# Rotary angles of the first layer: a transfer of their own, VectorE in place of GpSimd, and six matrix products on ones at the start

## The chip, the core and the metric

The kernel runs on one core of a Trainium2 chip. The metric is the device time of one execution in microseconds (us), the median of several runs. The engines are named as the profile names them: PE is TensorE's matmul, PEld its weight load, DVE is VectorE, ACT is ScalarE, POOL is GpSimd, SP is SyncE; a q behind a name is that engine's sequencer, which issues DMAs.

## The reference, cut to what matters

Four residual layers run over 256 positions of width 1024. A layer is a token mixer (layers 0 and 3: dilated attention in three head groups; layer 1: short convolution; layer 2: Conformer convolution) and a gated convolutional feed-forward block, each between RMS norms. The change touches only what feeds the rotary embedding of the attention layers:

```python
inv_freq = ROPE_THETA ** (-jnp.arange(0, ROT_DIM, 2, dtype=jnp.float32) / ROT_DIM)   # 8 frequencies
ang = positions.astype(jnp.float32)[..., None] * inv_freq                            # (256, 8)
cos, sin = jnp.cos(ang)[:, :, None, :], jnp.sin(ang)[:, :, None, :]
q = rope_partial(qkv[:, :, 0], cos, sin)
k = rope_partial(qkv[:, :, 1], cos, sin)
```

The angles reach 255 radians, so the kernel brings them into the range from -pi to pi before it takes sines.

## The kernel before

Activations stand transposed: 128 channels in partitions, 256 positions in the free dimension, eight such blocks (k = 0 to 7) for the width of 1024. Every fp32 product with a weight is made of three single-pass products (`mm3`, lines 280 to 282; in `value`, lines 894 to 896): high part of the weight with high and low part of the activation, low part of the weight with the high part.

**Weights** come as one stream (`Stream`): blocks `raw` of 1 MB, in three buffers, loaded by SP in the order of use (`load`; the first block in two halves). A block holds two pieces of 128x1024. ACT copies a piece to its high part `whi` (`first`, line 192), DVE subtracts to get the low part `wlo` (`second`, line 198). `st.copy()` and `st.diff()` place one such step each in the program; `take` hands the next piece to PE. A raw buffer is loaded anew when DVE has taken both of its pieces.

**Order.** All work is under a manual schedule: every engine runs its instructions in the order in which the code below issues them, and waits where an input is missing. A DMA also signals on one of eight counters, which the transfers share in turn: before SP issues a transfer, it waits until the earlier transfer on the same counter has landed. The order listings call the counters DMAHW0 to DMAHW7.

**The start** (lines 1112 to 1127): ACT's queue issues the first norm gains `par` and the positions `pi`; SP's queue issues the input `h`, the first weight blocks, the constants `cst` (identity, a block of 1/1024 named `ones`, and the 8 frequencies `freq` in the last columns), two more weight blocks, the masks `msk` and the other parameters.

**Layer 0, first steps.** `attention` (line 810) calls `rotary()`, then `boundary`, then `sines()`.

- `rotary` (line 1053) sets two tables to 1 and 0 on POOL and then does the angles, all on POOL: positions to fp32 (line 1068), times the frequencies (two instructions at line 1066), then three range steps (for e in 20, 10, 0) of eleven instructions each, 128x16 elements, each one dependent on the one ahead of it, and a clamp.
- `boundary` (line 356; here with `mg` None) makes high and low parts of the gained input: `hi` on ACT (line 291), `lo` on DVE (line 288). Between and behind them it places copies and diffs of the first weight pieces, and the squares for the norm (ACT, line 379). In the end DVE sums the squares (line 285, three sums of 128x512) and forms `acc` (line 288).
- `sines` (line 1089): two small DVE instructions (lines 288 and 1091), eight ACT sines (line 1095), a table load (line 1098).
- PE does four `column`s of 24 products (q and k of two head groups), then `value` (line 882): 24 products for the first 128 positions, and then the hook `before`: `rstd_of([acc])` (two products at line 306, whose result gives the norm factor by way of DVE and ACT), `turned` (four transposes of the tables at line 1104, copied to `ctab` and `stab` by ACT), and after it the 24 products for the other 128 positions, and the next column.

In each layer the feed-forward block then runs on PE as one long row of products (22 x 2 columns of 24, 14 slabs of 24, 8 tails of 24: 1,584 products).

## Time and profile before

| What | us |
|---|---|
| median of 3 runs | 1566.38 |
| the three runs | 1560.3, 1566.38, 1568.5 |
| the profiled execution, its own time | 1566.16 |
| its span (first to last instruction) | 1564.3 |
| around the span (1566.16 - 1564.3) | 1.86 |
| PE busy | 1538.2 (98%) |
| DVE busy | 1243.2 (79%) |
| ACT busy | 925.8 (59%) |
| POOL busy | 17.9 (1%) |

PE is busy for nearly the whole span, so a saving counts where PE stands still or runs slowly. Start times in the rows are us from the span's start. Matmuls are pipelined: how fast PE goes is read from the distance between their starts, not from how long each one lasts. `PEclk` is the granted share of TensorE's full clock, and has a value only where the trace holds a record of it.

### The profile page before, as it was taken

The numbers are of one execution on the slowest core, as the hardware profiler recorded it, in microseconds if no ns is written. First come the engines' busy times: TensorE is split into PE (matmuls) and PEld (weight loads), VectorE is DVE, ScalarE is ACT, GpSimd is POOL, SyncE is SP. The second block draws the span as 40 slices with busy tenths as digits, with TensorE's granted clock in tenths as the row PEclk, the third lists the DMA queues.
The fourth block names the chain that finished last, engine by engine and source line by source line (L and its number), as shares of the span: only waits on it lengthen the run. The fifth ranks groups of instructions, "written<-read, shape, count | busy, mean of one in ns | idle before, by whom it ended". The sixth has DMA issues, their size and how long they took to land.

```text
span 1564.3 us, 31521 instructions
## 1 busy us (share of the span) xinstructions
PE 1538.2 (98%) x13194; PEld 1501.4 (96%) x13194; DVE 1243.2 (79%) x2177; ACT 925.8 (59%) x1623; POOL 17.9 (1%) x51
## 2 busy tenths in 40 slices
PE   6999999999999999999999999999999999999998
PEld 6999999999999999999999999999999999999997
DVE  4997877698886779888699588896888778588783
ACT  6564645575574566656576666566546446565562
POOL 4000000000000000000000000000000000000000
PEclk9999999999999999999999999999999999999999
DMA  5663433266552644655333136553544334245540
GB/s 218 216 213 139 162 141 130 81 218 223 195 202 103 219 162 167 238 197 201 115 135 108 55 135 244 191 186 135 216 162 164 133 136 163 107 156 222 190 162 28
DMA packets 36718, 256.94 MB, mean 164 GB/s; under 512 B 4320, under 2 KB 4448, under 8 KB 5984
## 3 DMA queue, kind: packets, MB, share of 16 engines
q1 hardware_dynamic: 36288, 254.93, 45.2%
q8 instruction: 103, 1.69, 0.4%
q14 instruction: 39, 0.32, 0.1%
q10 hardware_dynamic: 288, 0.01, 0.0%
HBM read 253.87 MB, written 1.05 MB: 163 GB/s over the span
## 4 chain that ended last, share of the span: by engine, by line
PE 93%; DVE 3%; ACT 1%; POOL 1%; issue 1%; DMA 1%; DVEq 0%; ACTq 0%; POOLq 0%
PE psA L537 17%; PE psB L280 10%; PE psB L282 10%; PE psB L281 10%; PE psA L280 7%; PE psA L281 7%; PE psA L282 7%; PE psA L894 3%; PE psA L895 3%; PE psA L896 3%; PE psB L731 2%; PE psB L942 2%; PE psB L913 2%; PE psA L453 2%; PE psB L931 2%; PE psA L448 2%
## 5 line engine op out<-in xcount | busy, mean ns | idle before, releaser
L198 DVE TENSOR_TENSOR wlo<-raw,whi 128x1024 fp32r<-128x1024 f32 x480 | 580.2, 1220 | 34.6 <-ACT whi L192 33.9
L192 ACT CAST whi<-raw 128x1024 fp32r<-128x1024 f32 x480 | 491.1, 1049 | 22.8 <-DMA raw<-in_w_dram 17.2
L282 PE MATMUL psB<-act,wlo 128*128 128x256 f32 x1392 | 385.6, 277 | 0.0
L280 PE MATMUL psB<-act,whi 128*128 128x256 f32 x1392 | 385.6, 277 | 0.0
L281 PE MATMUL psB<-act,whi 128*128 128x256 f32 x1392 | 385.6, 277 | 0.0
L280 PE MATMUL psA<-act,whi 128*128 128x256 f32 x1040 | 298.6, 287 | 8.0 <-ACT whi L192 7.1
L282 PE MATMUL psA<-act,wlo 128*128 128x256 f32 x1040 | 290.0, 279 | 0.5 <-DVE wlo L198 0.5
L281 PE MATMUL psA<-act,whi 128*128 128x256 f32 x1040 | 290.1, 279 | 0.2
L537 PE MATMUL psA<-act,whi 128*128 128x256 f32 x1536 | 265.1, 277 | 0.0
L282 PEld LDWEIGHTS psB<-act,wlo 128*128 128x128 f32 x1392 | 262.5, 189 | 0.0
L281 PEld LDWEIGHTS psB<-act,whi 128*128 128x128 f32 x1392 | 261.3, 188 | 0.0
L280 PEld LDWEIGHTS psB<-act,whi 128*128 128x128 f32 x1392 | 261.3, 188 | 0.0
L537 PEld LDWEIGHTS psA<-act,whi 128*128 128x128 f32 x1536 | 231.7, 188 | 0.0
L537 PE MATMUL psA<-act,wlo 128*128 128x256 f32 x768 | 212.9, 277 | 0.0
L280 PEld LDWEIGHTS psA<-act,whi 128*128 128x128 f32 x1040 | 197.0, 189 | 13.6 <-ACT whi L192 7.1
L282 PEld LDWEIGHTS psA<-act,wlo 128*128 128x128 f32 x1040 | 196.9, 189 | 0.8 <-DVE wlo L198 0.8
L281 PEld LDWEIGHTS psA<-act,whi 128*128 128x128 f32 x1040 | 196.9, 189 | 0.6 <-DVE act L285 0.5
L291 ACT ACTIVATE tmp<-act,par 128x256 f32<-128x256 f32 x176 | 80.2, 503 | 161.7 <-DVE act L285 161.7
L288 DVE SCALAR_TENSOR_TENSOR tmp<-act,par,tmp 128x255 f32<-128x255 f32 (+1 forms) x352 | 146.6, 479 | 19.7 <-ACT tmp L291 19.7
L537 PEld LDWEIGHTS psA<-act,wlo 128*128 128x128 f32 x768 | 144.9, 189 | 0.0
L285 DVE TENSOR_TENSOR act<-psB,act 128x512 f32<-128x512 f32 (+2 forms) x94 | 58.5, 625 | 82.2 <-PE psB L282 45.3
L922 ACT ACTIVATE act<-act,tiny 128x512 f32<-128x512 f32 x64 | 46.4, 725 | 110.3 <-DVE tiny L920 110.3
(126 smaller groups left out, 2189.1 us busy)
## 6 DMA issues: line engine op xcount, KB each, us to landing
raw<-in_w_dram SPq DMA_DIRECT2D x239, 1024.0 KB, 4.8
h<-in_xT_dram SPq DMA_DIRECT2D x4, 256.0 KB, 5.0
raw<-in_w_dram SPq DMA_DIRECT2D x2, 512.0 KB, 5.5
out_dram<-h SPq DMA_DIRECT2D x4, 256.0 KB, 2.0
msk<-in_masks_dram SPq DMA_DIRECT2D x1, 512.0 KB, 9.4
par<-in_params_dram SPq DMA_DIRECT2D x1, 484.0 KB, 10.1
cst<-in_consts_dram SPq DMA_DIRECT2D x1, 132.0 KB, 5.9
par<-in_params_dram ACTq DMA_DIRECT2D x1, 4.0 KB, 2.9
```

Source lines behind the costliest of these rows:

```text
L192: self.nc.scalar.copy(out=hi, in_=raw)
L198: self.nc.vector.tensor_tensor(out=lo, in0=raw, in1=hi.bitcast(F32), op=ALU.subtract)
L280: nc.tensor.matmul(o, lhsT=whi, rhs=x[0], start=first, stop=False)
L281: nc.tensor.matmul(o, lhsT=whi, rhs=x[1], start=False, stop=False)
L282: nc.tensor.matmul(o, lhsT=wlo, rhs=x[0], start=False, stop=last)
L285: nc.vector.tensor_tensor(out=out, in0=a, in1=b, op=op)
L288: nc.vector.scalar_tensor_tensor(out=out, in0=a, scalar=s, in1=b, op0=op0, op1=op1)
L291: nc.scalar.activation(out=out, in_=a, func=AF.Identity, scale=s, bias=b)
L537: nc.tensor.matmul(o, lhsT=a, rhs=b, start=first and i == 0, stop=last and i == 2, skip_group_check=True)
L894: nc.tensor.matmul(oc, lhsT=xh, rhs=whi[:, k % 4, :], start=k == 0, stop=False)
L895: nc.tensor.matmul(oc, lhsT=xh, rhs=wlo[:, k % 4, :], start=False, stop=False)
L896: nc.tensor.matmul(oc, lhsT=xl, rhs=whi[:, k % 4, :], start=False, stop=k == KD - 1)
```

## The change

The frequencies get a third small transfer on ACT's queue; the transfer of `cst` on SP's queue leaves them out. The small tiles of the angles no longer come from the pool `tmp` but from a new tile `rot`. POOL still does the conversion and the two products with the frequencies. The three range steps and the clamp go to DVE. A product and a sum that were two POOL instructions are one on DVE (`STT`), so that a range step has seven instructions. The two small DVE instructions of `sines` go with the clamp. The whole is now a generator of four portions of 7, 7, 7 and 3 instructions; `boundary` calls it four times, each time behind one `st.diff()`. At the very beginning DVE sets a new tile `idle` to one, and PE does six fp32 products of 128x256 on it, whose result nobody reads.

```diff
--- before.py
+++ after.py
@@ -38,6 +38,7 @@
 FIRST = 10
 EVERY = 3
 LAG = 8
+HEAD = 6
 NCST = 2 * P + ROT // 2
 
 PCOLS = {}
@@ -245,6 +246,7 @@
     ident = cst[:, 0:P]
     ones = cst[:, P:2 * P]
     freq = cst[:, 2 * P:NCST]
+    rot = cp.tile([P, 8 * (ROT // 2)], F32, name="rot")
     msk = cp.tile([P, 2, 512], F32, name="msk")
     h2 = [cp.tile([P, 2, T], F32, name=f"h{k}") for k in range(KD // 2)]
     h = [h2[k // 2][:, k % 2, :] for k in range(KD)]
@@ -353,7 +355,7 @@
     def bc2(a):
         return a.rearrange("p (s t) -> p s t", s=1).to_broadcast([P, 2, T])
 
-    def boundary(mg, rb, gain, permuted=False):
+    def boundary(mg, rb, gain, permuted=False, beside=None):
 
 
         xs = [None] * KD
@@ -397,6 +399,7 @@
                 st.copy()
                 square(q)
                 st.diff()
+                next(beside)
             st.copy()
             st.diff()
         elif not gain:
@@ -808,8 +811,8 @@
     SWAP = [(i + 8) % 16 if i < 16 else i for i in range(32)]
 
     def attention(l, mg, rb):
-        sines, turned = rotary() if l == 0 else (None, None)
-        xs, acc = boundary(mg, rb, f"mpre{l}", True)
+        angles, sines, turned = rotary() if l == 0 else (None, None, None)
+        xs, acc = boundary(mg, rb, f"mpre{l}", True, angles)
         if l == 0:
             sines()
         ct, sn = act(), act()
@@ -1054,7 +1057,8 @@
 
 
         nf = ROT // 2
-        pf, ang, kf, a2 = tmp()[:, :2], tmp()[:, :2 * nf], tmp()[:, :2 * nf], tmp()[:, :2 * nf]
+        pf, ang, kf, a2 = (rot[:, i * 2 * nf:(i + 1) * 2 * nf] for i in range(4))
+        pf = pf[:, :2]
         tabs = [act()[:, :, :P] for _ in range(2)]
         for t, v in zip(tabs, (1.0, 0.0)):
             nc.gpsimd.memset(t, v)
@@ -1063,32 +1067,36 @@
 
         def TS(out, a, s1, op0, s2=None, op1=None):
             more = {} if op1 is None else {"op1": op1}
-            nc.gpsimd.tensor_scalar(out=out, in0=a, scalar1=s1, scalar2=s2, op0=op0, **more)
+            nc.vector.tensor_scalar(out=out, in0=a, scalar1=s1, scalar2=s2, op0=op0, **more)
 
         nc.gpsimd.tensor_copy(out=pf, in_=pi_)
         for c in range(2):
-            TS(ang[:, c * nf:(c + 1) * nf], freq, pf[:, c:c + 1], ALU.mult)
-        for e in (20, 10, 0):
-            period = two_pi * 2.0 ** e
-            parts, rest = [], period
-            for _ in range(3):
-                q = 2.0 ** (math.floor(math.log2(abs(rest))) - 12)
-                c = round(rest / q) * q
-                parts.append(c)
-                rest -= c
-            parts.append(float(np.float32(rest)))
-            TS(kf, ang, float(np.float32(1.0 / period)), ALU.mult)
-            TS(kf, kf, magic, ALU.add)
-            TS(kf, kf, -magic, ALU.add)
-            for c in parts:
-                TS(a2, kf, -c, ALU.mult)
-                nc.gpsimd.tensor_tensor(out=ang, in0=ang, in1=a2, op=ALU.add)
-        lim = float(np.nextafter(np.float32(math.pi), np.float32(0)))
-        TS(ang, ang, lim, ALU.min, -lim, ALU.max)
+            nc.gpsimd.tensor_scalar(out=ang[:, c * nf:(c + 1) * nf], in0=freq, scalar1=pf[:, c:c + 1], scalar2=None,
+                                    op0=ALU.mult)
+
+        def angles():
+            for e in (20, 10, 0):
+                period = two_pi * 2.0 ** e
+                parts, rest = [], period
+                for _ in range(3):
+                    q = 2.0 ** (math.floor(math.log2(abs(rest))) - 12)
+                    c = round(rest / q) * q
+                    parts.append(c)
+                    rest -= c
+                parts.append(float(np.float32(rest)))
+                TS(kf, ang, float(np.float32(1.0 / period)), ALU.mult)
+                TS(kf, kf, magic, ALU.add)
+                TS(kf, kf, -magic, ALU.add)
+                for c in parts:
+                    STT(ang, kf, -c, ang, ALU.mult, ALU.add)
+                yield
+            lim = float(np.nextafter(np.float32(math.pi), np.float32(0)))
+            TS(ang, ang, lim, ALU.min, -lim, ALU.max)
+            STT(a2, ang, -1.0, ang, ALU.mult, ALU.max)
+            TS(a2, a2, -1.0, ALU.mult, math.pi / 2, ALU.add)
+            yield
 
         def sines():
-            STT(a2, ang, -1.0, ang, ALU.mult, ALU.max)
-            nc.vector.tensor_scalar(out=a2, in0=a2, scalar1=-1.0, scalar2=math.pi / 2, op0=ALU.mult, op1=ALU.add)
             for t, a, sign in zip(tabs, (a2, ang), (1.0, -1.0)):
                 for half in range(2):
                     for r in range(2):
@@ -1107,13 +1115,19 @@
                 nc.scalar.copy(out=tab[:, 1, :], in_=oi)
                 scaled(tab[:, 0, :], oi, -1.0 / math.sqrt(DH))
 
-        return sines, turned
+        return angles(), sines, turned
 
     with tc.manual_schedule():
         pi_ = cp.tile([P, 2], I32, name="pi")
         nc.scalar.dma_start(out=par[:, 0:KD], in_=params[:, 0:KD])
         nc.scalar.dma_start(out=pi_, in_=pos)
+        nc.scalar.dma_start(out=freq, in_=consts[:, 2 * P:NCST])
         nc.scalar.preload_act_table(AF.Sin)
+        idle = act()
+        nc.vector.memset(idle, 1.0)
+        o = psum("B")[:, :T]
+        for _ in range(HEAD):
+            nc.tensor.matmul(o, lhsT=idle[:, 0, :P], rhs=idle[:, 1, :], start=True, stop=True)
         nc.sync.dma_start(out=h2[0], in_=xT[0])
 
         def rest():
@@ -1121,7 +1135,7 @@
                 nc.sync.dma_start(out=h2[q], in_=xT[q])
 
         st.load(1, rest)
-        nc.sync.dma_start(out=cst, in_=consts)
+        nc.sync.dma_start(out=cst[:, :2 * P], in_=consts[:, :2 * P])
         st.load(3)
         nc.sync.dma_start(out=msk, in_=masks)
         nc.sync.dma_start(out=par[:, KD:], in_=params[:, KD:])
```

What stands in a row on DVE before, from the last low part of the input on: five diffs of weight pieces, the sums of the squares, and then the two instructions of `sines` (tmp_102 is the angle tile) and the first one of the norm factor.

```order
L288 SCALAR_TENSOR_TENSOR act_170<-h_77,par,act_170 128x256
L198 TENSOR_TENSOR wlo<-raw,whi 128x1024 x5
L285 TENSOR_TENSOR act_177<-act_177,act_186 128x512
L285 TENSOR_TENSOR act_177<-act_177,act_193 128x512
L285 TENSOR_TENSOR act_177<-act_177,act_202 128x512
L288 SCALAR_TENSOR_TENSOR tmp_213<-act_177 128x256
L288 SCALAR_TENSOR_TENSOR tmp_104<-tmp_102 128x16
L1091 TENSOR_SCALAR tmp_104<-tmp_104 128x16
L309 RECIPROCAL tiny_359<-psS_356 128x2
```

The same place now, from the third portion on (rot holds the angles; lines 1070 and 290 are the helpers TS and STT; the two portions ahead of it read like the third):

```order
L199 TENSOR_TENSOR wlo<-raw,whi 128x1024
L1070 TENSOR_SCALAR rot<-rot 128x16 x3
L290 SCALAR_TENSOR_TENSOR rot<-rot 128x16 x4
L199 TENSOR_TENSOR wlo<-raw,whi 128x1024
L1070 TENSOR_SCALAR rot<-rot 128x16
L290 SCALAR_TENSOR_TENSOR rot<-rot 128x16
L1070 TENSOR_SCALAR rot<-rot 128x16
L199 TENSOR_TENSOR wlo<-raw,whi 128x1024
L287 TENSOR_TENSOR act_150<-act_150,act_166 128x512
L287 TENSOR_TENSOR act_150<-act_150,act_180 128x512
L287 TENSOR_TENSOR act_150<-act_150,act_196 128x512
L290 SCALAR_TENSOR_TENSOR tmp_210<-act_150 128x256
```

A portion now stands between one diff and the next, four times, ahead of the sums; the two instructions behind the sums are gone.

What stands on SP's queue at the start, before, from the second half of the first weight block on:

```order
L180 DMA raw<-in_w_dram 128x1024
L1124 DMA cst<-in_consts_dram 128x264 [waits DMAHW0_49]
L182 DMA raw<-in_w_dram 128x2048 [waits DMAHW1_49]
L182 DMA raw<-in_w_dram 128x2048 [waits DMAHW2_49]
L1126 DMA msk<-in_masks_dram 128x1024 [waits DMAHW3_49]
L1127 DMA par<-in_params_dram 128x968 [waits DMAHW4_49]
```

And now:

```order
L181 DMA raw<-in_w_dram 128x1024 [waits DMAHW0_49]
L1138 DMA cst<-in_consts_dram 128x256 [waits DMAHW1_49]
L183 DMA raw<-in_w_dram 128x2048 [waits DMAHW2_49]
L183 DMA raw<-in_w_dram 128x2048 [waits DMAHW3_49]
L1140 DMA msk<-in_masks_dram 128x1024 [waits DMAHW4_49]
L1141 DMA par<-in_params_dram 128x968 [waits DMAHW5_49]
```

The transfers stand in the same order, but one more transfer ahead of them has moved each by one counter. The first of these, which waited for nothing, now waits on a counter used by one of the first two transfers (`par` or the first `h`). Counter 2 belongs to `pi`: the transfer behind `cst` now waits for it, where before it was the one after. Counter 4, on which `msk` now waits, belongs to the frequencies.

## Rows read from the trace of the kernel before

**Rows 1.** Waits, first 50 us: engine line, releaser: us in all, times, longest.

```profile
PE psA L280 <- ACT whi L192: 7.1, 1, 7.1
...
PE psB L1104 <- ACT act L1095: 5.1, 1, 5.1
...
DVE tmp L288 <- POOL tmp L1066: 4.7, 1, 4.7
```

**Rows 2.** Windows: stretch and length, busy us of PE, PEld, DVE, ACT, POOL, PEclk, DMA.

```profile
25.00:30.00 5.00, 0.12 (x1) 0.15 (x2) 0.42 (x3) 0.80 (x8) 2.75 (x12) 0.74 0.13 52
30.00:35.00 5.00, 5.00 (x27) 4.87 (x28) 1.65 (x5) 4.94 (x10) 0.00 (x0) 0.58 0.00 0
```

**Rows 3.** Timeline, PE: start, us, engine, line, operation, tiles, count, idle before.

```profile
13.78 0.28 PE L280 MATMUL psA<-act,whi 128*128 128x256 f32 x1
...
21.60 0.28 PE L894 MATMUL psA<-whi,act 128*128 128x256 f32 x1
...
24.33 0.50 PE L306 MATMUL psS<-cst,tmp 128*128 128x1 f32 x4
29.88 1.09 PE L1104 MATMUL psB<-cst,act 128*128 128x128 f32 x4 [5.05 <-ACT act L1095]
30.62 0.56 PE L894 MATMUL psA<-whi,act 128*128 128x256 f32 x1
...
35.13 0.29 PE L280 MATMUL psA<-act,whi 128*128 128x256 f32 x1
```

**Rows 4.** Timeline, POOL, start of the kernel.

```profile
9.75 1.57 POOL L1066 TENSOR_SCALAR tmp<-cst,tmp 128x8 f32<-128x8 f32 x2 [3.38 <-DMA cst<-in_consts_dram]
...
28.49 0.20 POOL L1066 TENSOR_SCALAR tmp<-tmp 128x16 f32<-128x16 f32 x1
```

**Rows 5.** Timeline, ACT, 19 to 36 us.

```profile
19.22 1.05 ACT L192 CAST whi<-raw 128x1024 fp32r<-128x1024 f32 x1
29.20 0.96 ACT L1095 ACTIVATE act<-tmp 128x16 f32<-128x16 f32 x8 [8.93 <-DVE tiny L309]
...
33.69 1.28 ACT L869 ACT_TABLE_LOAD   x1
35.33 0.84 ACT L291 ACTIVATE act<-psA,tiny 128x256 f32<-128x256 f32 x2 [0.36 <-PE psA L896]
```

**Rows 6.** Timeline, DVE, 11 to 30 us.

```profile
11.95 1.23 DVE L198 TENSOR_TENSOR wlo<-raw,whi 128x1024 fp32r<-128x1024 f32 x1
14.05 1.22 DVE L198 TENSOR_TENSOR wlo<-raw,whi 128x1024 fp32r<-128x1024 f32 x1 [0.88 <-ACT whi L192]
...
21.45 2.16 DVE L285 TENSOR_TENSOR act<-act,act 128x512 f32<-128x512 f32 x3
23.64 0.43 DVE L288 SCALAR_TENSOR_TENSOR tmp<-act 128x256 f32<-128x256 f32 x1
28.72 0.18 DVE L288 SCALAR_TENSOR_TENSOR tmp<-tmp 128x16 f32<-128x16 f32 x1 [4.65 <-POOL tmp L1066]
28.93 0.17 DVE L1091 TENSOR_SCALAR tmp<-tmp 128x16 f32<-128x16 f32 x1
29.02 0.16 DVE L309 RECIPROCAL tiny<-psS 128x2 f32<-128x2 f32 x1
```

**Rows 7.** Timeline, PE, fp32 products of 128x256 (two records each).

```profile
295.36 1.89 PE L331 MATMUL psB<-cst 128*128 128x256 f32 x8
```

**Rows 8.** DMA issues, first 30 us: operation, count, KB each, median us to landing.

```profile
raw<-in_w_dram SPq DMA_DIRECT2D x5, 1024.0 KB, 6.3
...
pi<-in_pos_dram ACTq DMA_DIRECT2D x1, 1.0 KB, 5.0
```

**Rows 9.** Windows, a short idle of PE in layer 3.

```profile
1094.00:1098.00 4.00, 3.10 (x27) 2.90 (x25) 2.51 (x9) 1.84 (x4) 0.00 (x0) 1.00 0.00 0
```

**Rows 10.** Windows, PE in the feed-forward blocks of layers 0 and 3.

```profile
320.00:440.00 120.00, 120.00 (x1061) 120.00 (x1061) 105.28 (x169) 74.86 (x117) 0.00 (x0) 1.00 0.60 212
...
1400.00:1520.00 120.00, 120.00 (x1021) 120.00 (x1020) 101.16 (x164) 72.18 (x113) 0.00 (x0) 1.00 0.56 202
```

## The prediction, made before the changed kernel was run

> **What bounds the kernel now.** PE is busy for 98% of the span, so I first looked for the places where it is not. The waits of the first 50 us [rows 1] show two: PE's first product starts at 7.1 us, held by ACT's copy of the first weight piece, and later PE stands still for 5.1 us before the transposes of the rotary tables. Who is late there is read backwards through the rows. The transposes wait for ACT's eight sines (29.20 us), these for two DVE instructions (28.72 and 28.93), and these for POOL, whose clamp ends at 28.69 [rows 3 to 6]. DVE had nothing to do for 4.7 us before that. POOL started on the angles at 9.75, when the frequencies had landed, and took until then: 36 instructions in a chain, 34 of them on 128x16 elements from 11.4 on, 0.51 us each on average [rows 4].
>
> The idle costs more than its 5 us. Its window, 25 to 30 us, has a granted clock of 0.74, the next one 0.58 [rows 2]: in it TensorE falls from its upper level (2.4 GHz) to the lower (1.2 GHz). So the four transposes take 0.74 us from first start to the next product (29.88 to 30.62), and the 24 products behind them 4.51 us (30.62 to 35.13). The 24 products of the same kind ahead of the hook, at the full clock, took 2.73 us (21.60 to 24.33) [rows 3]. The start of the kernel looks alike: the trace has no clock record there, but from 13.78 on 93 products take 10.55 us until 24.33, 0.113 us each [rows 3], and before that they stand about twice as far apart.
>
> **The angle steps on DVE: what they cost.** The change takes 33 of the POOL instructions away and puts 22 in their place on DVE, together with the two that were there already: portions of 7, 7, 7 and 3. Each instruction depends on the one ahead. The nearest row is the pair in `sines`, of the same form and size: starts 28.72 and 28.93, so 0.21 us per dependent step; an independent one follows 0.09 us later [rows 6]. A portion of seven is 6 x 0.21 + 0.09 = 1.35 us, the last one 2 x 0.21 + 0.09 = 0.51 us.
>
> They stand between the diffs of weight pieces, where DVE waits for ACT: the first of four such waits is 0.88 us [rows 6], the others are 0.84 to 0.87. With the 0.08 us by which instructions overlap (the sums start at 21.45, the diff ahead of them ends at 21.53), there is room for 0.95 us. Three portions are too long by 0.40 us each, the fourth gives 0.40 back: the sums are late by 0.80 us. `acc` was ready at 23.64 + 0.43 = 24.07 and is now ready at 24.87. Its reader on PE, at line 306, came at 24.33 without waiting [rows 3, 6]. Now it comes at about 24.93, after a short wait of PE.
>
> Queued behind the portions on DVE are the diffs of the next pieces. PE takes them later than they are ready in each case: with PE at 0.113 us per product from 13.2 us on, the four diffs behind a portion end some 0.1 to 0.4 us before the product that reads them. That is thin, but any loss here comes out of the same wait for `acc`, not on top of it.
>
> Below this there is the case that the portions hide wholly: `acc` at 24.07, 0.8 us better. Above it stands POOL's own price, 0.51 us per instruction: portions of 3.57 and 1.53 us, `acc` later by 3 x 2.62 + 0.61 = 8.5 us. I take 0.21, since its row is the same operation on the same engine.
>
> The Trainium skill (VectorE: DVE Perf Modes, section "The DRAIN you can't avoid") says that the next VectorE instruction does not start until the pipe of the one ahead is empty, and that leaving out the wait between two gains nothing. The rows speak against that here: the independent one at 29.02 starts while the one ahead still runs until 29.10 [rows 6]. By the page every step would cost 0.21 us, the sum four times 0.12 us more, and the gain below would be 6.1 instead of 6.6 us.
>
> **What goes away.** The sines no longer wait for POOL. The fourth portion ends near 21.2 us; ACT finishes its copy at 19.22 + 1.05 = 20.27, so the sines (0.96 us) run from about 21.3 to 22.2, and the transposes are no longer held by them [rows 5]. PE's next sequence is the two products at line 306 from 24.93 (0.50 us), the transposes, and 24 products. PE's idle is now about 1 us at most. A window in layer 3 with 0.9 us of idle in 4 us still has the clock at 1.00 [rows 9], so I take the full clock: transposes 0.37, half of 0.74; products 2.73. The next column starts at 24.93 + 0.50 + 0.37 + 2.73 = 28.53, where it was 35.13: **6.6 us earlier**. If the clock fell all the same, 0.37 + 1.78 = 2.15 us of this would be lost.
>
> What is late next: ACT's copies of the tables and its table load (1.28 us, 33.69 to 34.97) come ahead of the scaling of `value`, which waited 0.36 us for PE [rows 5]. In the new order ACT copies at 22.2 + 1.28 to 24.5, takes the table copies behind the transposes at about 25.9, and ends the load near 28.4, when PE ends the products. It is a tie, worth 0.3 us at most. Behind it the order on every engine is what it was, with the same distances, and the saving stays until the end: nothing in the stream runs by an outside time, and the blocks needed next are issued before.
>
> **The transfers.** The frequencies land by a small transfer; the nearest row is `pi`, 1 KB, 5.0 us [rows 8]. Issued at about 1.6 us they land at 6.6, at 10 even if they queue twice as long. POOL's two products (1.57 us) [rows 4] are done before 11.6; DVE asks at 13.1. On SP's queue everything is moved by one counter: the second half of block 0 waits until about 3.6 us (landing of a first transfer), the second block until `pi` lands, near 6.1. Weight blocks took 6.3 us from issue to landing there [rows 8], so it lands by 12.4; ACT copies it at 13.0, ahead of the diff at 14.05 [rows 6]. `msk` and the parameters behind it wait for the frequencies, and nobody needs them before some tens of us. Cost nothing; if the second block were late by 1 us, `acc` would be late by as much.
>
> **The six products.** Eight records of such products, four of them, take 1.89 us [rows 7]; six are 12 records, 2.8 us, or 5.7 at half the clock. Behind a fill of DVE (0.72 us, the price of one 128x512 sum [rows 6]) they are over before 7.1, under PE's wait for the first copy. They let the first column run at the full clock, but its second piece is ready only at 11.95 + 1.23 = 13.18 [rows 6], so PE gains at most 0.5 us by 24.33, and `acc` is later than that. With the angle steps in, they are worth nothing, between 0 and 0.1 us.
>
> **Sum.** 1564.3 - 6.6 = 1557.7 for the span; with the 1.86 us around it **1559.6 us**, against 1566.16 for the profiled execution, which lies 0.2 us under the median.
>
> **The rivals.** *Another pace of PE in the feed-forward blocks.* In layer 0 a stretch of 120 us holds 1,061 products, in layer 3 only 1,021, both with PE without a gap and the clock at 1.00 [rows 10]: 113.1 and 117.5 ns. Layers 1 and 2 go as layer 0. Nothing in the code differs, so a stretch seems to keep the pace at which it begins. Over 1,584 products that is 7.0 us per layer, about the distance of the lowest run (1560.3) from the others. The change shifts every beginning. If layer 3 goes at the quick pace, the time is 1559.6 - 7.0 = 1552.6. If one more block goes at the slow one, it is 1566.6, no change. If two or more more go slow, it is 1573.6 and above: **slower than before**, from the second block on, and past 0.5% with little more.
>
> *DVE as slow as POOL.* At 0.51 us per step `acc` comes at 32.6, 7.7 us later than forecast, and after such an idle the clock is down, 2.15 us: 1569.4, slower. From about 0.40 us per step on the change loses. The row of 0.21 speaks against it.
>
> *The clock falls in the short wait.* 1559.6 + 2.15 = 1561.8; the window of layer 3 speaks against it.
>
> **How the numbers follow.** 0.5% of 1566 is 7.8 us, about what a measurement of this kernel can tell from no change. Chances: forecast, 1559.6 with bounds of 1558.5 and 1561: 0.47. Quick pace in layer 3: 0.22. One more slow block: 0.13. Clock falls: 0.10. Two or more slow blocks: 0.05. DVE like POOL: 0.03. Faster by over 0.5% are the quick pace and the part of the forecast with its best bound and a median that falls well, 0.12: 0.34 in all. Slower by over 0.5% is 0.04, most of the slow blocks. The rest, 0.62, is within. The range goes from 1553 (half of the quick pace left out) to 1566.5 (slow blocks left out).
>
> **What would show it.** In the profile of the changed kernel: on DVE, portions of about 1.35 us between diffs and the sums' end near 24.9; on ACT, sines near 21.3; on PE, line 306 near 24.9 with an idle of about 1 us before it, transposes right behind, the next column at 28.5, no clock below 1.00 between 14 and 40 us; 12 records of idle products over before 7.1. Wrong it is if a dependent DVE step takes much more than 0.21 us, if PE's idle at `acc` costs the clock, or if the feed-forward blocks change their pace: then the start shows the 6.6 us and the end does not.

## The result, and the profile after

| | before | after |
|---|---|---|
| runs beside each other, us | 1560.3, 1566.38, 1567.33, 1568.5 | 1550.05, 1551.44, 1551.7, 1552.87 |
| median, us | 1566.86 | 1551.57 |
| profiled execution, us | 1566.16 | 1551.44 |
| span of the profiled execution, us | 1564.3 | 1549.7 |

The ratio is 0.9922, 95% interval 0.9894 to 0.9949: the changed kernel is faster by 0.8%, more than the 0.5% that a measurement of this kernel can tell from no change (the two medians alone give 0.9902). The time lies 8.0 us under the forecast and 1.4 us under the range's low end. It lies 1.0 us under the time that the rival of the quick pace gave (1552.6).

The runs of before lie in two groups, one near 1560 us (the lower) and one near 1567.5 us (the upper), and this ratio compares a mixture of them with one group. The experiments below add 75 runs of before in four series, and the groups return in each.

**The start.** Rows of PE in the kernel after (columns as in [rows 3]):

```profile
1.45 5.49 PE L1130 MATMUL psB<-act 128*128 128x256 f32 x12 [1.45 <-DVE act L1127]
7.00 0.58 PE L282 MATMUL psA<-act,whi 128*128 128x256 f32 x1
...
24.65 0.61 PE L308 MATMUL psS<-cst,tmp 128*128 128x1 f32 x4 [0.63 <-DVE tmp L290]
25.12 0.64 PE L1112 MATMUL psB<-cst,act 128*128 128x128 f32 x4
25.51 0.36 PE L897 MATMUL psA<-whi,act 128*128 128x256 f32 x1
...
28.42 0.28 PE L282 MATMUL psA<-act,whi 128*128 128x256 f32 x1
```

The idle of 5.05 us in [rows 3] is gone; 0.63 us is left, and it stands before the products that read `acc` (line 308 now), as foretold. The transposes follow at once. The column behind `value` starts at 28.42 us where it was 35.13: 6.71 us earlier.

DVE in the kernel after (columns as in [rows 6]): a portion stands between two diffs (line 199).

```profile
11.80 1.23 DVE L199 TENSOR_TENSOR wlo<-raw,whi 128x1024 fp32r<-128x1024 f32 x1
12.94 0.58 DVE L1070 TENSOR_SCALAR rot<-rot 128x16 f32<-128x16 f32 x3
13.56 0.80 DVE L290 SCALAR_TENSOR_TENSOR rot<-rot 128x16 f32<-128x16 f32 x4
14.28 1.22 DVE L199 TENSOR_TENSOR wlo<-raw,whi 128x1024 fp32r<-128x1024 f32 x1
...
20.37 0.17 DVE L1070 TENSOR_SCALAR rot<-rot 128x16 f32<-128x16 f32 x1
20.57 0.17 DVE L290 SCALAR_TENSOR_TENSOR rot<-rot 128x16 f32<-128x16 f32 x1
20.78 0.17 DVE L1070 TENSOR_SCALAR rot<-rot 128x16 f32<-128x16 f32 x1
20.86 1.22 DVE L199 TENSOR_TENSOR wlo<-raw,whi 128x1024 fp32r<-128x1024 f32 x1
22.00 2.14 DVE L287 TENSOR_TENSOR act<-act,act 128x512 f32<-128x512 f32 x3
24.17 0.43 DVE L290 SCALAR_TENSOR_TENSOR tmp<-act 128x256 f32<-128x256 f32 x1
```

Seven steps take 1.34 us from their first start to the next diff (12.94 to 14.28). Dependent steps start 0.20 to 0.21 us apart (20.37, 20.57, 20.78), and the independent diff 0.08 us behind the last of them, while that one still runs. The Trainium skill (VectorE: DVE Perf Modes, section "The DRAIN you can't avoid") says that the next instruction does not start until the pipe is empty, and in the same paragraph that one that is not held starts earlier. The trace agrees with the second, with the 0.08 us of the diff; the prediction told only the first.

Two windows of the kernel after, one at the start and one in the last feed-forward block (columns as in [rows 2] and [rows 10]):

```profile
25.00:30.00 5.00, 5.00 (x45) 5.00 (x45) 1.82 (x6) 4.05 (x9) 0.00 (x0) 1.00 0.24 98
30.00:35.00 5.00, 5.00 (x45) 5.00 (x45) 4.58 (x5) 4.18 (x5) 0.00 (x0) 1.00 0.45 151
1400.00:1520.00 120.00, 120.00 (x1061) 120.00 (x1061) 102.90 (x166) 74.13 (x115) 0.00 (x0) 1.00 0.53 188
```

The granted clock stays at 1.00, the upper level, where [rows 2] have 0.74 and 0.58. The last window answers to the second of [rows 10]: 1,061 products in 120 us where there were 1,021. Layer 3's feed-forward block now goes at the quick pace (0.113 us per product, where the slow one is 0.118).

**Where the 14.6 us of span come from.** The same ACT instruction in both kernels, at the entry of the last feed-forward block and near its end (start, us, engine, line, operation, tiles). Kernel before:

```profile
1363.82 0.91 ACT L291 ACTIVATE act<-h,par 128x256 fp32r<-128x256 f32 x2 [2.57 <-DVE h L285]
...
1544.91 0.47 ACT L291 ACTIVATE act<-psA,par 128x256 f32<-128x256 f32 x1
```

Kernel after:

```profile
1356.52 0.91 ACT L293 ACTIVATE act<-h,par 128x256 fp32r<-128x256 f32 x2 [2.57 <-DVE h L287]
...
1530.98 0.47 ACT L293 ACTIVATE act<-psA,par 128x256 f32<-128x256 f32 x1
```

At the entry the kernel after is 7.30 us ahead, near the end 13.93. So 6.6 us were won in this block alone, where the change has no instruction. Of the 7.3 us ahead of it, 6.7 are there at 28 us. Another part, some 0.8 us by PE's starts (6.51 us ahead at 850.96, 7.28 at 862.60), is won at the end of the Conformer mixer of layer 2: there a window of before, and then the matching one of after (columns as in [rows 2]), read

```profile
866.00:871.00 5.00, 5.00 (x22) 4.31 (x22) 2.46 (x9) 3.22 (x6) 0.00 (x0) 0.66 0.01 3
```

```profile
859.00:864.00 5.00, 4.72 (x31) 4.04 (x31) 2.46 (x9) 3.51 (x7) 0.00 (x0) 1.00 0.00 0
```

The granted clock was 0.66 there before and is 1.00 after. This part need not belong to the change: e8 below, in which only the last block differs from before, has 1.00 there too, and between before and its second trace (e5) the entry of the last block moves by 2.0 us (1363.82 and 1365.80) although the column behind `value` starts at 35.13 and 35.09.

Three questions stay: which part of the change makes the 6.7 us, whether the other two are needed, and why the last block went quick.

### The profile page after: what moved, and what is told of

Read it like the earlier page. It is cut to its first block, busy times and chain, and to the rows that moved or that the text cites. A ratio compares the mean times of both kernels' runs of the same rounds, so it can differ in the third digit from the quotient of the medians.

```text
span 1549.7 us, 31536 instructions
## 1 busy us (share of the span) xinstructions
PE 1532.4 (99%) x13206; PEld 1493.1 (96%) x13206; DVE 1246.3 (80%) x2200; ACT 925.4 (60%) x1623; POOL 3.8 (0%) x17
## 4 chain that ended last, share of the span: by engine, by line
PE 94%; DVE 4%; ACT 1%; issue 1%; DMA 0%; DVEq 0%; SPq 0%; ACTq 0%
PE psA L540 17%; PE psB L284 10%; PE psB L283 10%; PE psB L282 10%; PE psA L282 7%; PE psA L283 7%; PE psA L284 7%; PE psA L897 3%; PE psA L898 3%; PE psA L899 3%; PE psB L734 2%; PE psB L945 2%; PE psB L916 2%; PE psA L456 2%; PE psB L934 2%; PE psA L451 2%
```

## The experiments

Each ratio is to runs of before in the same series, with its 95% interval, also where the edit is shown against after.

The four runs of after are quick and those of before mostly are not. Theory A at the outset: the six products take a buffer of the rotating kinds `act` and PSUM "B", so every later tile stands in another buffer, and that sets the block's pace. Theory B: the pace is set by something else, a matter of timing or chance at the block's beginning.

### e1: the products alone

Against the kernel before:

```diff
+        idle = act()
+        nc.vector.memset(idle, 1.0)
+        o = psum("B")[:, :T]
+        for _ in range(6):
+            nc.tensor.matmul(o, lhsT=idle[:, 0, :P], rhs=idle[:, 1, :], start=True, stop=True)
         nc.sync.dma_start(out=h2[0], in_=xT[0])
```

> The kernel before plus the six products on ones alone (and with them one more tile of the rotating activation tiles and one more bank B taken at the start). Start theory (what bounds is POOL's chain of angles): the columns run at the full clock, but the transposes still wait for the sines at 29.2 us, and the next column starts at 35.1 us as before; gain at the start 0. Two theories for the 7 us by which the last feed-forward block became shorter in the changed kernel (0.113 instead of 0.118 us per product): (A) the shift of the rotating tiles by one decides the pace: then this kernel has the quick pace too, 1559 to 1560 us; (B) the moment at which PE begins decides: behind 35 us this kernel runs like the one before, 1566 us.

Measured: 1559.67 us (1557.65 to 1560.74, ten runs), ratio 0.9978 [0.9958, 0.9998]. PE in e1, and its window in the last block:

```profile
23.62 0.61 PE L307 MATMUL psS<-cst,tmp 128*128 128x1 f32 x4
29.34 1.09 PE L1105 MATMUL psB<-cst,act 128*128 128x128 f32 x4 [5.12 <-ACT act L1096]
```

```profile
1400.00:1520.00 120.00, 120.00 (x1062) 120.00 (x1061) 104.11 (x170) 74.23 (x117) 0.00 (x0) 1.00 0.56 202
```

PE comes to `acc` 0.7 us earlier than in [rows 3] and then waits for the sines as before: the transposes are earlier by 0.5 us (29.34 for 29.88), the column behind by 0.2 (34.91 for 35.13). The start of before itself moves by as much (35.09 to 35.79 in e5, e8 and e11, which leave it as it was or nearly so). So the products do nothing for the start. But all ten runs lie in the lower group, and the traced one has the quick pace.

### e2: the change without the products

Against the kernel after:

```diff
-        idle = act()
-        nc.vector.memset(idle, 1.0)
-        o = psum("B")[:, :T]
-        for _ in range(HEAD):
-            nc.tensor.matmul(o, lhsT=idle[:, 0, :P], rhs=idle[:, 1, :], start=True, stop=True)
```

> The changed kernel without the six products on ones (so the rotating activation tiles and banks B stand as before; the tile for the angles and the four tmp tiles fewer stay). Start theory: the sums of squares set the end of the first stretch, not the products; the second half of the clock's ramp is hidden; line 306 still at 24.7 us, next column at 28.4 to 28.6 us, gain at the start 6.5 to 6.7 us. A rival at the start: without them the first columns run at half clock until some 13.7 us and end at 24.3, which is still ahead of the sums, so at most 0.2 us lost. Pace theory A (tiles): the last block is slow again, 1558 to 1560 us. Pace theory B (moment): it stays quick, 1551 to 1553 us.

Measured: 1553.54 us (1552.24 to 1554.29, seven runs), ratio 0.993 [0.991, 0.995]. The next column starts at 28.75, 0.33 us later than in after; the last block is quick, with 1,061 products in the window. So the products are not needed for the quick pace either. The other 1.6 us or so of the median lie between layers 1 and 3: e2's trace is 2.6 us behind after at the entry of the last block (1359.11 for 1356.52), and it has the fall of the clock at the Conformer mixer. The two traces of before differ by 2.0 us at that entry, so that these runs don't tell what the products do there.

### e3: the transfer alone

Against the kernel before:

```diff
         nc.scalar.dma_start(out=pi_, in_=pos)
+        nc.scalar.dma_start(out=freq, in_=consts[:, 2 * P:NCST])
...
-        nc.sync.dma_start(out=cst, in_=consts)
+        nc.sync.dma_start(out=cst[:, :2 * P], in_=consts[:, :2 * P])
```

> The kernel before plus the frequencies' own transfer alone; the angles stay on POOL. They land at 6.8 instead of 9.6 us, so POOL begins 2.7 us earlier and ends its clamp near 26 us; sines at 26.5, transposes near 27. If TensorE's clock still falls in the idle of some 2.4 us: next column at 32.4, gain at the start 2.7 us; if the clock holds: 30.3, gain 4.8 us. Whole time 1561 to 1563.5 us with the last feed-forward block at the slow pace, 7 us less at the quick one. Pace theory A (tiles stand as before): slow.

Measured: 1558.38 us (1557.25 to 1559.41, ten runs), ratio 0.9958 [0.994, 0.9975]. PE and one window of e3:

```profile
28.08 1.09 PE L1104 MATMUL psB<-cst,act 128*128 128x128 f32 x4 [3.50 <-ACT act L1095]
```

```profile
25.00:30.00 5.00, 1.92 (x9) 1.82 (x10) 0.42 (x3) 2.57 (x10) 1.38 (x7) 0.77 0.11 44
```

POOL starts on the angles 2.7 us earlier (7.07 for 9.75) and ends only 1.8 us earlier (26.89 for 28.69). In the stretch gained its steps stand beside a busy DVE, where single ones take longer in e9 below; that this makes the missing 0.9 us was not measured. PE still waits 3.50 us, the clock still falls, and the next column comes at 32.77, 2.36 us earlier than before. The chain on POOL is what had to go. The traced last block is quick here too, and all ten runs lie in the lower group.

### e4: the change, with the products on buffers that are there anyway

Against the kernel after:

```diff
-        idle = act()
-        nc.vector.memset(idle, 1.0)
-        o = psum("B")[:, :T]
+        nc.vector.memset(ctab, 1.0)
+        o = psum("S")[:, :T]
...
-            nc.tensor.matmul(o, lhsT=idle[:, 0, :P], rhs=idle[:, 1, :], start=True, stop=True)
+            nc.tensor.matmul(o, lhsT=ctab[:, 0, :P], rhs=ctab[:, 1, :], start=True, stop=True)
```

> The changed kernel with the six products on a tile of the tables that is free at that time and with another bank as output, so that the rotating activation tiles and the banks B stand as in the kernel before, and all times are those of the changed kernel. Start theory: next column at 28.4 us as in the changed kernel. Pace theory A (the shift by one decides): last block slow, 1558 to 1559 us. Pace theory B (the moment decides): quick, 1551 to 1552 us.

Measured: 1551.94 us (1551.11 to 1553.51, five runs), ratio 0.9922 [0.9895, 0.9949]; next column at 28.50, quick pace (1,061). `act` and "B" rotate as in before now (as in e2), and the time is that of after. Theory A falls for the changed kernel.

### e5: the kernel before once more

> The kernel before, unchanged, for a second trace and more runs on the same chip beside the others. Its 23 runs so far lie in two heaps, nine near 1559.6 us and most of the others near 1567.5 us, while each variant so far keeps to one heap. If the pace of the last feed-forward block (7 us) is what parts them, a run near 1559.6 has about 1,061 products in the 120 us from 1400 us on and one near 1567.5 has 1,021. If the heaps come from something else, a trace near 1559.6 shows 1,021 there as well.

Measured: 1559.56, 1560.03, 1560.55, 1560.6, 1561.47 and 1566.5, 1566.53, 1567.62, 1568.13, 1568.28 us; ratio 0.9999 [0.9977, 1.0021]. Five runs in each group and none in the five microseconds between them. The traced run (1568.13) has the slow pace in the last block:

```profile
1400.00:1520.00 120.00, 120.00 (x1021) 120.00 (x1020) 101.13 (x164) 71.71 (x113) 0.00 (x0) 1.00 0.56 201
```

### e6: all steps in one row on DVE

Against the kernel after, in `boundary`:

```diff
                 st.diff()
-                next(beside)
             st.copy()
             st.diff()
+            for _ in beside:
+                pass
```

> The changed kernel with all 24 angle steps in one row on DVE between the last diff and the sums of squares, in place of four portions between the diffs. Start theory (0.21 us per dependent step, in portions hidden in waits of DVE for ACT): the 24 steps take 23 x 0.21 + 0.09 = 4.9 us, nothing of it hidden; acc comes at 28.7 instead of 24.6 us, PE stands still for 4.5 us, the clock falls (it did in an idle of 3.5 us), and the next column starts at 34.3 to 34.7 instead of 28.4 us: 1557 to 1558.5 us. Rival: the clock holds, next column at 32.5 us, 1555.5 us. Rival: the place makes no difference, since the diffs and not the steps set the end: 1551.6 us.

Measured: 1559.27 us (1559.05 to 1559.69, seven runs), ratio 0.9965 [0.9947, 0.9983]. PE and the two windows of e6:

```profile
29.35 0.67 PE L308 MATMUL psS<-cst,tmp 128*128 128x1 f32 x4 [4.35 <-DVE tmp L290]
```

```profile
25.00:30.00 5.00, 0.65 (x5) 0.65 (x6) 3.92 (x13) 3.09 (x10) 0.00 (x0) 0.97 0.23 92
30.00:35.00 5.00, 5.00 (x32) 5.00 (x32) 1.82 (x6) 2.98 (x8) 0.00 (x0) 0.68 0.00 0
```

The same 24 steps, at the same 0.20 to 0.21 us each, ahead of the sums instead of between the diffs: `acc` at 29.30 instead of 24.60, PE idle for 4.35 us, the clock falls to the lower level for part of the next stretch, and the next column starts at 34.68, 6.3 us later than in after. It is the portions, fitted into DVE's waits for ACT, that make the steps nearly free. All but 0.45 us of the start's 6.71 hangs on them.

### e7: the change without the transfer

Against the kernel after:

```diff
-        nc.scalar.dma_start(out=freq, in_=consts[:, 2 * P:NCST])
...
-        nc.sync.dma_start(out=cst[:, :2 * P], in_=consts[:, :2 * P])
+        nc.sync.dma_start(out=cst, in_=consts)
```

> The changed kernel without the frequencies' own transfer: they come with the constants again, landing near 9.6 us. Start theory: POOL's two products end by 11.7 us, DVE asks for them at 12.9 us, so nothing is lost: next column at 28.4 us, 1551 to 1552.5 us. Rival: POOL beside a busy DVE ends later than 12.9 us, and each microsecond of that is lost once: 1552.5 to 1554 us.

Measured: 1552.44 us (1551.07 to 1552.87, four runs), ratio 0.9914 [0.9892, 0.9936]; next column at 28.41, quick pace (1,061). POOL's two products now run from 9.60 to 11.75, and DVE asks for them at 12.92: the later landing is hidden whole. With the angles on DVE the transfer of its own is worth nothing.

### e8: a break inside the last block

Against the kernel before, in the feed-forward block, ahead of the ninth pair of columns of the last layer:

```diff
             if what == "col":
+                if i == 8 and l == DEPTH - 1:
+                    pause = psum("S")[:, :P]
+                    for _ in range(2):
+                        nc.tensor.matmul(pause, lhsT=ident, rhs=ident, start=True, stop=True)
```

> The kernel before plus two small fp32 products (128x128, four records, some 0.4 us) ahead of the ninth pair of columns of the last feed-forward block alone. Theory (PE keeps the pace with which a row of products begins until something breaks the row): a run that enters the block at the slow pace can change to the quick one at the break, some 50 us into the block, so that the slow heap of the kernel before moves down by up to 5 us, or is gone, and a trace shows 0.118 us per product ahead of the break and 0.113 behind it, or the other way round. Rival (something that lasts for the whole block, as the place of its data, sets the pace): two heaps as before, at 1560 and 1568 us, and the same pace on both sides of the break.

Measured: 1563.46 us (ten runs: 1559.5, 1561.11, 1561.32, and seven from 1562.84 to 1564.77), ratio 0.9984 [0.9967, 1.0001]. The two added products in e8, and windows on both sides of them:

```profile
1425.20 0.61 PE L609 MATMUL psS<-cst 128*128 128x128 f32 x4
```

```profile
1380.00:1420.00 40.00, 40.00 (x342) 40.00 (x341) 39.42 (x65) 28.44 (x44) 0.00 (x0) 1.00 0.63 220
1430.00:1470.00 40.00, 40.00 (x356) 40.00 (x355) 31.63 (x50) 22.91 (x35) 0.00 (x0) 1.00 0.50 174
```

40 us hold 342 products ahead of the break and 356 behind it, 0.117 and 0.112 us each; the change stands at the break (over longer stretches 0.118 and 0.113). PE has no gap on either side and the clock is 1.00 on both. The slow traces without the break (before, e5, e10) keep 0.118 us over the whole 120 us shown. So the row keeps the pace at which it runs, and two small products of another shape let it go over to the quick one. The seven upper runs lie near 1563.8, where before's upper group lies near 1567.5: some 4 of the 7 us, with the break about a third of the way in. The traced run (1561.32) is not one of the seven, and it was slow until the break all the same; for this kernel the time alone does not tell how the block began.

### e9: the first range step on POOL

Against the kernel after, in `rotary`; the added lines are the eleven instructions of e = 20 on POOL:

```diff
+        PS(kf, ang, float(np.float32(1.0 / period)), ALU.mult)
+        PS(kf, kf, magic, ALU.add)
+        PS(kf, kf, -magic, ALU.add)
+        for c in parts:
+            PS(a2, kf, -c, ALU.mult)
+            nc.gpsimd.tensor_tensor(out=ang, in0=ang, in1=a2, op=ALU.add)
+
         def angles():
-            for e in (20, 10, 0):
+            yield
+            for e in (10, 0):
```

> The changed kernel with the first of the three range steps (eleven instructions) left on POOL, which is free from 8.9 us on, and the other two and the clamp on DVE in three portions behind the second to the fourth of the four diffs. Start theory: DVE has seven dependent steps less (1.4 us), so acc comes at 23.2 to 23.7 instead of 24.6 us and PE, which ends its products at 24.0, no longer waits for it (0.63 us in the changed kernel): next column at 27.8 instead of 28.4 us, whole time 1550.5 to 1551.5 us. Rival: POOL, at some 0.6 us per step beside a busy DVE, ends its step after 15.2 us, and DVE waits for it with the diffs queued behind: next column at 28.4 us or later.

Measured: 1553.23 us (1551.96 to 1553.63, four runs), ratio 0.9914 [0.9891, 0.9938]. POOL, then DVE, then PE in e9:

```profile
11.85 1.31 POOL L1087 TENSOR_SCALAR rot<-rot 128x16 f32<-128x16 f32 x1
13.25 0.22 POOL L1094 TENSOR_TENSOR rot<-rot 128x16 f32<-128x16 f32 x1
13.56 0.25 POOL L1087 TENSOR_SCALAR rot<-rot 128x16 f32<-128x16 f32 x1
13.89 1.30 POOL L1094 TENSOR_TENSOR rot<-rot 128x16 f32<-128x16 f32 x1
```

```profile
15.87 0.59 DVE L1070 TENSOR_SCALAR rot<-rot 128x16 f32<-128x16 f32 x3 [0.76 <-POOL rot L1094]
```

```profile
25.13 0.49 PE L308 MATMUL psS<-cst,tmp 128*128 128x1 f32 x3 [0.95 <-DVE tmp L290]
```

My expectation failed and its rival was right. POOL took from 9.01 to 15.84 for the eleven, 0.6 us each, and two of them, at 11.85 and 13.89, lasted 1.3 us instead of 0.25 while DVE ran a diff beside them (11.83 and 13.89). DVE waited 0.76 us for POOL, `acc` came 0.47 us later than in after, and the next column at 28.90. Nothing is to be had from sharing the steps in this way.

### e10: the angles on DVE alone

Against the kernel after:

```diff
-        nc.scalar.dma_start(out=freq, in_=consts[:, 2 * P:NCST])
-        idle = act()
-        nc.vector.memset(idle, 1.0)
-        o = psum("B")[:, :T]
-        for _ in range(HEAD):
-            nc.tensor.matmul(o, lhsT=idle[:, 0, :P], rhs=idle[:, 1, :], start=True, stop=True)
...
-        nc.sync.dma_start(out=cst[:, :2 * P], in_=consts[:, :2 * P])
+        nc.sync.dma_start(out=cst, in_=consts)
```

> The kernel before with the angle steps on DVE alone: neither the frequencies' own transfer nor the six products. Start theory: the steps on DVE bring the whole gain at the start, the products 0.3 us at most and the transfer nothing: next column at 28.5 to 28.9 us, whole time 1552 to 1554 us with the quick pace in the last block. Rival (the parts need each other): without the transfer and the products the next column comes after 29.5 us.

Measured: 1559.16 us (nine runs: 1552.89, 1554.7, and seven from 1558.09 to 1560.59), ratio 0.9948 [0.9929, 0.9967]. The start has the whole gain: `acc` at 24.74, next column at 28.57, 6.56 us earlier than before. But the traced run's last block is slow:

```profile
1400.00:1520.00 120.00, 120.00 (x1021) 120.00 (x1021) 100.57 (x165) 71.38 (x113) 0.00 (x0) 1.00 0.53 192
```

Here the two gains stand apart. Its median is what the forecast said (1559.6), for the reason that the forecast gave: 6.6 us at the start, the last block as it was. Two of nine runs are lower by some 6 us and reach the times of after.

### e11: the kernel before with one fill more

Against the kernel before:

```diff
+        nc.gpsimd.memset(tabs[1], 0.0)
```

> The kernel before with one more fill of a table half on POOL at the very beginning, 0.3 us in which POOL waits for the positions anyway: one instruction more, no time moved. For the two heaps of the kernel before, near 1560 and 1567.5 us. Theory (the moment at which PE reaches the last block, set by the start, decides the pace): nothing moves, so two heaps as before, a median anywhere between 1560 and 1568 us. Rival (any change of the instruction streams moves it): one heap at 1559 to 1560.5 us, as in the other variants.

Measured: 1566.02 us (ten runs: 1560.62, 1561.22, 1561.29, and seven from 1565.56 to 1568.57), ratio 0.9997 [0.9977, 1.0017]. A shift that nobody waits for leaves both groups as they are. The traced run is one of the lower group (1561.22), and its last block is quick:

```profile
1400.00:1520.00 120.00, 120.00 (x1061) 120.00 (x1060) 104.63 (x168) 73.45 (x116) 0.00 (x0) 1.00 0.58 205
```

With e5 that ties the groups to the pace: columns at 35.55 and 35.09, the same entry into the last block (1365.80 us in both traces), and 6.9 us between the two executions. The lower group of the unchanged kernel itself was not traced.

### e12: the kernel before with e4's products

Against the kernel before:

```diff
+        nc.vector.memset(ctab, 1.0)
+        o = psum("S")[:, :T]
+        for _ in range(6):
+            nc.tensor.matmul(o, lhsT=ctab[:, 0, :P], rhs=ctab[:, 1, :], start=True, stop=True)
```

> The kernel before plus the six products alone, on a tile of the tables that is free at that time and with another bank as output, so that the rotating activation tiles and banks B stand as before. At the start nothing is gained (next column at 34.6 to 35.1 us). So far every kernel with the products or with the frequencies' own transfer lies in one heap (the quick pace in the last block), and every kernel with neither lies in two (the one before, the one with a break, angles only, one more fill). Theory (the products themselves, or PE's longer stream, keep the slow pace away): one heap, 1558.5 to 1560.5 us. Rival (in the kernel with the products only it was the shift of the rotating tiles and banks by one): two heaps at 1560 and 1567.5 us.

Measured: 1559.02 us (nine runs from 1558.56 to 1560.99, one at 1565.94), ratio 0.9997 [0.9979, 1.0014]; traced run quick. That looks like e1, but in this series before itself was in the lower group in 10 of 12 runs (median 1559.27). The times decide nothing between the two theories.

## Why the prediction was right and wrong

**Right: the chain of waits and its price.** The working said that POOL's chain holds the sines, that these hold PE, and that the idle takes the clock with it. e3 (chain shorter by 1.8 us, still 3.50 us of idle, clock still down) and e10 (chain off POOL, idle and fall gone) show it from both sides. The gain of the start was worked out as 6.6 us; it is 6.71 in after and 6.56 in e10. Step by step:

| step | foretold | after |
|---|---|---|
| frequencies landed, us | 6.6 | 6.78 |
| seven dependent steps, us | 1.35 | 1.34 |
| last portion, us | 0.51 | 0.49 |
| sines start | 21.3 | 21.05 |
| `acc` ready | 24.87 | 24.60 |
| products that read it | 24.93 | 24.65 |
| PE's idle ahead of them | about 1 | 0.63 |
| 24 products behind the transposes, us | 2.73 | 2.91 |
| next column | 28.53 | 28.42 |

Two terms are off and go against each other. `acc` came 0.27 us earlier: the first of the diffs started at 11.80 instead of 11.95 [rows 6], and from it to the sums DVE went without a wait, a portion and a diff taking 2.48 us where 2.50 was foretold. The 24 products took 0.18 us more, at 0.121 us each instead of 0.114. The rival in which a DVE step costs as much as one of POOL, and the one in which the clock falls in the short wait, are both out: 0.21 us per step, clock 1.00. Two slips in the working change nothing: 34 POOL instructions went, not 33 (the clamp goes too), and at POOL's price the fourth portion would cost 0.58 us, not 0.61. The 6.1 us that the prediction gave by the page leave out that page's sentence on an instruction that starts earlier.

**Right for the start: the transfer and the products cost nothing.** The transfer is worth nothing beside the angles on DVE (e7). The products were put at 0 to 0.1 us; without them the next column is 0.33 us later (e2) or 0.15 us (e10), so up to three times as much, and still nothing that the median could show. Behind the start it is otherwise, as told below: with either of them the last block was quick in every run by the times (e2, e7), with neither it was slow in seven of nine (e10).

**Right: the gain is kept.** In e10 the 6.6 us of the start appear in the median as far as the groups let one see it (1559.16 for 1566.9, or 1552.9 to 1554.7 for about 1559.6).

**Wrong: the last step, the weighing of the rivals.** The forecast took it that layer 3's feed-forward block keeps its slow pace, chance 0.47, with the quick pace at 0.22. The quick pace came, in all four runs by their times, and with it 6.6 us (7.0 foretold). The mechanism was right as written: 117.5 against 113.1 ns per product without a gap and at the full granted clock, kept along a row (e8). The mistake was in the reading of the runs of before. Three runs were shown, 1560.3, 1566.38 and 1568.5; the working noted that the lowest stood off by the price of one block, but the sum went from the profiled execution, which was one of the upper group, as if its pace were fixed by the kernel. The runs of before have both (the two groups, with the traces of e5 and e11). A forecast from the lower group, 1560.3 - 6.6 = 1553.7, was as near at hand, and the range should have reached below it.

So the 15.3 us between the medians hold 6.7 us of the change's start, which is certain, and 6.6 us of pace, which before has in a part of its own runs and the change, by the traces below, in all that were made. What is left is within the groups' own width; some 0.8 us of it is the Conformer mixer, where after, e4 and e7 are without the fall of the clock and e2, e9 and e10 have it. Against before's lower group (about 1559.6 us) the change is worth some 8 us, 0.5%; against the upper one (about 1567.5) some 16.

**Partly open: why the last block goes at the one pace or the other.** Over the first three series, with the four runs of after, none of 51 runs of after, e1, e2, e3, e4, e6, e7 and e9 had the slow pace, by their times; all of these carry the products or the transfer. Before, e5, e8, e10 and e11, which carry neither, had it in half of their runs or more (before in 40 of 63). But in the last series before itself had the quick one in 10 of 12 runs, and e12 in 9 of 10, so that a tally of one series shows little.

The traces tell more. Ahead of the long row the norm factor is worked out: DVE takes a reciprocal, ACT a root, DVE forms the factor, and four small products on PE spread it. In e5 (slow), e11 (quick) and e1 (quick) these rows read

```profile
1377.88 0.17 DVE L309 RECIPROCAL tiny<-psS 128x2 f32<-128x2 f32 x1 [1.48 <-PE psS L306]
...
1378.42 0.17 ACT L310 ACTIVATE tiny<-psS 128x2 f32<-128x2 f32 x1 [4.16 <-DVE tiny L309]
...
1379.15 0.28 PE L282 MATMUL psA<-act,wlo 128*128 128x256 f32 x1
...
1379.33 0.68 PE L324 MATMUL psS<-cst,tiny 128*128 128x128 f32 x4
```

```profile
1377.57 0.17 DVE L309 RECIPROCAL tiny<-psS 128x2 f32<-128x2 f32 x1 [1.16 <-PE psS L306]
...
1378.12 0.17 ACT L310 ACTIVATE tiny<-psS 128x2 f32<-128x2 f32 x1 [3.84 <-DVE tiny L309]
...
1378.89 0.28 PE L282 MATMUL psA<-act,wlo 128*128 128x256 f32 x1
...
1379.02 0.68 PE L324 MATMUL psS<-cst,tiny 128*128 128x128 f32 x4
```

```profile
1375.52 0.17 DVE L310 RECIPROCAL tiny<-psS 128x2 f32<-128x2 f32 x1 [1.48 <-PE psS L307]
...
1375.78 0.17 ACT L311 ACTIVATE tiny<-psS 128x2 f32<-128x2 f32 x1 [3.88 <-DVE tiny L310]
...
1376.79 0.28 PE L283 MATMUL psA<-act,wlo 128*128 128x256 f32 x1
...
1376.90 0.60 PE L325 MATMUL psS<-cst,tiny 128*128 128x128 f32 x4
```

In the traces of before, e5, e8, e10, e11 and e12 ACT's root starts 0.54 to 0.55 us behind the reciprocal, in the other eight 0.26 to 0.27. These are the kernels in which slow runs occur at all, and those in which none does. In the four slow traces (before, e5, e8, e10) PE then stands for some 0.06 us, too short to be printed as idle: its four products come 0.18 us behind the product ahead of them. In e11 and e12 PE itself comes later and the distance is 0.13, in the eight others 0.11 to 0.12; all ten are quick. So the slow pace stood behind this short wait in four of four traces, and never without it. ACT's lateness goes together with the loading of code: in the six traces the instruction queue (q14 in the view of DMAs) starts 8 KB 1.2 us behind the reciprocal, in the eight others 8.2 to 8.5 us ahead of it. That the wait makes the pace is not shown, since no run added or took away only the wait; nor is it known how the loading delays the root, or why the transfer moves it, and so do the products in e1 and e7, but not those of e12.

Three things are ruled out as the cause alone. The rotation of tiles is not needed for the quick pace (e4). The time of arrival does not set it: e7 and e10 start alike (28.41 and 28.57) and differ, and e5 and e11 begin the block's products at 1366.35 and 1366.37 and differ. Nor does the chip, since the third and the fourth series ran on the same one, with 4 of 18 and 10 of 12 runs of before in the lower group.

Of the kernels that ran, none beats the changed one: e4 and e7 are equal to it, e9 is not better.

## What to carry to other kernels

A chain of small dependent steps belongs on the engine with the shortest step (here 0.21 us on DVE, 0.51 on POOL), cut into portions that fit that engine's own waits: placed so, 24 steps cost 0.6 us of PE's time here, and the same 24 in one row cost 6.3 us more. Before a forecast, look at the single runs, not only at their median: where they fall into two groups as far apart as one long stage of the kernel can be quick or slow, forecast from each group, and give the range both. What a part of a change is worth is found only by runs that take it out: transfer and products bought nothing measurable at the start, and yet the kernel without both (e10) is 7.6 us slower in the median, by the pace of a block that the change does not touch. A wait too short to be printed as idle can stand ahead of such a loss, so compare starts, row by row, between a quick and a slow trace.

## What the runs showed of the hardware

- A long row of 128x256 products with a weight load each runs at one of two paces, 0.113 or 0.118 us, with PE without a gap and the granted clock at 1.00 in both; it keeps its pace and changed it at a break of two small fp32 products (e8). Over the last block's 1,584 products that is 6.6 to 7 us. The runs of before show both by their times. The slow pace stood behind a wait of PE of some 0.06 us in all four slow traces.
- The idle of PE that kept the clock was 0.63 us in after, 0.66 in e10 and 0.95 in e9; 3.50 us (e3), 4.35 (e6) and 5.05 (before) lost it. But the clock also fell without an idle: at the end of the Conformer mixer of before PE ran 20 products of one column in 2.37 us (from 863.75) and went on with no idle that the view prints, and the window shown above has 0.66; after and e8 have the same rows and kept 1.00.
- POOL's 128x16 steps took 0.22 to 0.25 us alone, and single ones 1.3 us beside a diff of DVE (e9); its chain came to 0.51 us per step in before and 0.62 in e9.
- At the very start six fp32 products of 128x256 took 5.49 us in twelve records, about twice per record what [rows 7] show (0.46 for 0.24 us), as at the lower of TensorE's two levels; the trace has no clock record for that stretch, and its windows print 1.00 there all the same.
